# Storing the first output tile in four pieces as they are computed, in a SiLU-gate kernel

## The chip, the cores and the metric

The kernel runs on one core of a Trainium2 chip. The metric is the device time of one execution in microseconds (us), as the median of several executions. The span that a profile shows is about 1.8 us shorter than that time.

## The reference

```python
def setup_inputs():
    return {'x': np.random.randn(32, 512, 2048).astype(np.float32)}

def reference(x):
    half_dim = x.shape[-1] // 2
    x1, x2 = x[..., :half_dim].copy(), x[..., half_dim:].copy()
    silu_x1 = x1 * (1 / (1 + np.exp(-x1)))
    return (silu_x1 * x2).astype(np.float32)
```

There are 16384 rows of 8 KB that come in and 16384 rows of 4 KB that go out: 134.2 MB read and 67.1 MB written, with one SiLU and one multiply per output element.

## The kernel before

The rows are cut into 16 tiles. A tile gives each of the 128 partitions K = 8 neighbouring rows, so one partition's share of a load is one contiguous run of 64 KB in memory, and its share of a whole store is one run of 32 KB. There are two input buffers (`xt`) and two output buffers (`ot`). ScalarE (ACT) computes the SiLU, VectorE (DVE) the multiply, both in chunks of KC = 2 rows. ACT's queue issues the loads, SyncE's (SP) the stores. The last tile alone is stored chunk by chunk, in runs of 8 KB.

```python
    K = 8
    KC = 2
    ...
    in_pool = ctx.enter_context(tc.tile_pool(name="in_pool", bufs=2))
    out_pool = ctx.enter_context(tc.tile_pool(name="out_pool", bufs=2))
    ...
    def load(i):
        xt = in_pool.tile([P, K, in_cols], dt, name="xt")
        nc.scalar.dma_start(out=xt[:, :plan[i][1], :], in_=view(x_flat, i))
        loaded[i] = xt

    load(0)
    load(1)
    for i in range(n_tiles):
        k = plan[i][1]
        xt = loaded.pop(i)
        last = i == n_tiles - 1
        ov = view(out_flat, i)
        ot = out_pool.tile([P, K, half], dt, name="ot")
        for c in range(0, k, KC):
            ce = min(c + KC, k)
            nc.scalar.activation(out=ot[:, c:ce, :], in_=xt[:, c:ce, :half],
                                 func=mybir.ActivationFunctionType.Silu)
            nc.vector.tensor_mul(out=ot[:, c:ce, :], in0=ot[:, c:ce, :],
                                 in1=xt[:, c:ce, half:])
            if last:
                nc.sync.dma_start(out=ov[:, c:ce, :], in_=ot[:, c:ce, :])
        if not last:
            nc.sync.dma_start(out=ov, in_=ot[:, :k, :])
        if i + 2 < n_tiles:
            load(i + 2)
```

Load i+2 overwrites the input buffer of tile i, so it is issued when tile i has been computed. Tile i+2 writes the output buffer of tile i, so its first SiLU waits until store i has landed, all of it.

## Time and profile before

| | before |
|---|---|
| median time | 470.84 us (470.56 to 471.13, three runs) |
| span of the profiled execution | 468.9 us |
| one 64 KB load packet on one engine | 2.42 us |
| one 32 KB store packet | 1.21 us |
| one 8 KB store packet | 0.31 us |
| packets of one engine, added up at these durations | about 465 us |
| first tile's store: issued, landed | 32.7 us, 66.2 us |

Lines of the profile page of the kernel before. The DMA row gives the mean busy share of the 16 DMA engines in 40 slices of the span, in tenths; the line with percentages is the chain of waits by line; in the last three lines the numbers are the count, the size of each and the median time from issue to landing.

```profile
span 468.9 us, 269 instructions
...
DVE 142.3 (30%) x64; ACT 118.2 (25%) x65; POOL 0.2 (0%) x4
...
DMA  9899999999999998999999999999999989999998
...
DMA packets 5042, 201.35 MB, mean 429 GB/s; under 512 B 560, under 2 KB 560, under 8 KB 560
...
DMA xt<-in_x_dram 80%; DVE ot L92 15%; ACT ot L87 3%; DVEq L128 0%
...
out_dram<-ot SPq DMA_DIRECT2D x15, 4096.0 KB, 39.8
out_dram<-ot SPq DMA_DIRECT2D x4, 1024.0 KB, 5.7
xt<-in_x_dram ACTq DMA_DIRECT2D x16, 47.1
```

The engines that compute are idle for over two thirds of the span, and the DMA row has no hole. The kernel is bound by data movement. Reading the DMA row more finely: the trace has a record of each packet (start, duration, size, queue). The records do not name the engine, but each packet begins within some 4 ns of the end of another, so one engine's sequence can be followed from end to start. One DMA engine's packets, in order of time, look like this in the kernel before (L is the load queue, S the store queue, the number after it is the size in KB, the bracket is the duration in us):

```
38.88 S32(1.21)  40.09 L64(2.42)  42.50 S32(1.21)  43.72 S32(1.21)  44.93 L64(2.42)
47.34 S32(1.21)  48.55 L64(2.42)  50.96 S32(1.21)  52.17 L64(2.42)  54.59 S32(1.21)
```

Each packet starts when the one before it ends, and the two queues take turns, one packet each. (Where the store queue goes twice, at 42.50 and 43.72 us, a load had just ended: its 4-byte completion packet took the load queue's turn.)

Two more views of the kernel before: the waits (who waited for what; total us, times, longest us), and the timeline of tiles 0 to 2 (start, duration, instruction, count, and in brackets the idle time before it with what ended it; a line with x3 or x4 stands for several instructions, from the first one's start to the last one's end).

```profile
ACT ot L87 <- DMA xt<-in_x_dram: 338.8, 16, 22.1
DVE ot L92 <- ACT ot L87: 319.5, 16, 23.8
```

```profile
23.82 8.90 DVE L92 TENSOR_TENSOR ot<-ot,xt 128x2048 f32<-128x2048 f32 x4 [23.82 <-ACT ot L87]
32.74 51.99 SPq L100 DMA_DIRECT2D out_dram<-ot  x3
32.75 0.35 ACTq L74 DMA_DIRECT2D xt<-in_x_dram  x1
44.54 7.31 ACT L87 ACTIVATE ot<-xt 128x2048 f32<-128x2048 f32 x4 [15.36 <-DMA xt<-in_x_dram]
...
73.53 7.31 ACT L87 ACTIVATE ot<-xt 128x2048 f32<-128x2048 f32 x4 [21.68 <-DMA xt<-in_x_dram]
75.47 8.90 DVE L92 TENSOR_TENSOR ot<-ot,xt 128x2048 f32<-128x2048 f32 x4 [20.09 <-ACT ot L87]
84.40 0.37 ACTq L74 DMA_DIRECT2D xt<-in_x_dram  x1
```

ACT waits for loads alone, in all 16 tiles. Tile 2 starts at 73.53 us when its load lands; its output buffer has been free since 66.2 us.

### The profile page before, as it was taken

Reading aid. Unit: us, or ns where it says so; the run is one execution under the profiler, and the core shown is the slowest. Engines: PE = TensorE matmul, PEld = TensorE weight load, DVE = VectorE, ACT = ScalarE, POOL = GpSimd, SP = SyncE. Lnnn points to the kernel's source line nnn. Section 1 sums busy time; section 2 is a strip of 40 time slices with the busy share of each in tenths; the row PEclk is TensorE's granted clock in tenths of the full one; section 3 lists DMA queues with packets and bytes.
Section 4 is the critical chain, followed back from the end, with each engine's and each line's share of the span. In section 5 each row is a group of like instructions: output and inputs, shape, how many; then the busy total and the mean of one; then the engine's idle time right before and its main releaser. Section 6 shows DMA issues by size and latency. Waiting matters only on the chain.

```text
span 468.9 us, 269 instructions
## 1 busy us (share of the span) xinstructions
DVE 142.3 (30%) x64; ACT 118.2 (25%) x65; POOL 0.2 (0%) x4
## 2 busy tenths in 40 slices
DVE  0070705106061160601507025070250702407034
ACT  1142406023060330603206032060420604106051
POOL 0000000000000000000000000000000000000000
DMA  9899999999999998999999999999999989999998
GB/s 431 375 447 403 447 447 447 403 419 431 447 447 403 447 492 363 442 492 391 458 403 439 456 447 403 409 442 447 447 403 444 467 386 447 442 419 481 400 409 354
DMA packets 5042, 201.35 MB, mean 429 GB/s; under 512 B 560, under 2 KB 560, under 8 KB 560
## 3 DMA queue, kind: packets, MB, share of 16 engines
q10 hardware_dynamic: 2304, 134.22, 66.4%
q1 hardware_dynamic: 2736, 67.11, 33.2%
q14 instruction: 2, 0.02, 0.0%
HBM read 134.22 MB, written 67.11 MB: 429 GB/s over the span
## 4 chain that ended last, share of the span: by engine, by line
DMA 80%; DVE 15%; ACT 3%; DVEq 0%; issue 0%
DMA xt<-in_x_dram 80%; DVE ot L92 15%; ACT ot L87 3%; DVEq L128 0%
## 5 line engine op out<-in xcount | busy, mean ns | idle before, releaser
L92 DVE TENSOR_TENSOR ot<-ot,xt 128x2048 f32<-128x2048 f32 x64 | 142.3, 2286 | 319.5 <-ACT ot L87 319.5
L87 ACT ACTIVATE ot<-xt 128x2048 f32<-128x2048 f32 x64 | 116.9, 1897 | 338.8 <-DMA xt<-in_x_dram 338.8
L87 ACT ACT_TABLE_LOAD x1 | 1.3, 1283 | 1.3 <-PEq L117 1.3
L117 POOL MEMSET const-uint8-127<- 128x1 uint8 x1 | 0.1, 102 | 0.0
L117 POOL MEMSET const-bfloat16-1.0<- 128x1 bf16 x1 | 0.1, 101 | 0.0
L117 POOL MEMSET const-float32-0.0<- 128x1 f32 x1 | 0.1, 98 | 0.2 <-issue 0.2
L117 POOL MEMSET const-float32-1.0<- 128x1 f32 x1 | 0.1, 98 | 0.0
## 6 DMA issues: line engine op xcount, KB each, us to landing
out_dram<-ot SPq DMA_DIRECT2D x15, 4096.0 KB, 39.8
out_dram<-ot SPq DMA_DIRECT2D x4, 1024.0 KB, 5.7
xt<-in_x_dram ACTq DMA_DIRECT2D x16, 47.1
```

The source lines that it names most:

```text
L87: nc.scalar.activation(out=ot[:, c:ce, :], in_=xt[:, c:ce, :half], func=mybir.ActivationFunctionType.Silu,)
L92: nc.vector.tensor_mul(out=ot[:, c:ce, :], in0=ot[:, c:ce, :], in1=xt[:, c:ce, half:],)
L117: nc = _bacc.Bacc("TRN2", target_bir_lowering=False, num_devices=1)
```

## The change

The last tile's way of storing is used for the first tile too, so that the first store can begin at about 26 us, when two rows per partition are ready, and not at 32.7 us.

```diff
-        last = i == n_tiles - 1
+        in_pieces = i in (0, n_tiles - 1)
 [...]
-            if last:
+            if in_pieces:
                 nc.sync.dma_start(out=ov[:, c:ce, :], in_=ot[:, c:ce, :])
-        if not last:
+        if not in_pieces:
             nc.sync.dma_start(out=ov, in_=ot[:, :k, :])
```

## The prediction

> **What bounds the kernel now.** Data movement. The profile page's DMA row stands at 9 in nearly every slice, at a mean of 429 GB/s; DVE is busy 30%, ACT 25%; the chain of waits is 80% DMA of xt. The trace's DMA packet records say it more finely: a load moves 64 KB per packet (2.42 us on an engine), a tile store 32 KB (1.21 us), a last-tile piece 8 KB (0.31 us). Per engine that is 128, 120 and 32 packets: 309.5 + 145.6 + 9.9 = 465 us of a 468.9 us span. At most 4 us could be won, so a gain over 2% is out of reach.
>
> In steady state the two queues take strict turns, one load packet and one store packet, 3.63 us together: 2:1, just the ratio in which the kernel needs bytes. Both queues are always filled (a tile takes 29 us; a load lands after 47 us, a store after 40). The Trainium skill ("DMA: Bandwidth & Descriptors", section Queues, rings and completion order) says the engines go round robin between queues by packets of typically 9 to 17 descriptors. The trace agrees with the turns, but a turn here is one 64 KB or 32 KB run.
>
> **What the change does.** Bytes, compute (1.89 us per SiLU, 2.28 us per multiply) and instruction order on ACT and DVE stay. SP issues three more stores (0.33 us each, off the path). The first store can start at 26 us rather than 32.7. But the engines are full of loads then, so an early store only displaces a load.
>
> The harm: the pieces have 8 KB runs, so store 0 is 32 packets per engine instead of 8. If each turn is one packet, it gets 8 KB for every 64 KB of load. From about 31.5 us (3 packets left of load 1, 8 each of loads 2 and 3) there are 19 turns of 2.73 us, to about 84 us, with only 19 of 32 store packets out. The other 13 follow at 0.31 us. Store 0 lands at 88 to 91 us instead of 66.2.
>
> Tile 2 writes into tile 0's output buffer; the built program makes its first SiLU wait for all four pieces. Its input lands near 64 us, so ACT waits about 25 us, and load 4 cannot be issued. The load queue runs dry. Most of the stall is free: the loads ran ahead, and store 1 (8 x 1.21 = 9.7 us) then has the engines alone. After store 0 lands, tile 2 takes 10.9 us, and load 4 starts 1 to 2 us after issue. DMA idle: landing 0.5 to 2 + 10.9 + 1 to 2 - 9.7, so 2.7 to 5.2 us. Nothing later wins it back.
>
> **Predicted time: 474.3 us**, 80% range 470.4 to 477.2. Chances: faster by over 2% 0.01, within 2% 0.96, slower by over 2% 0.03.
>
> **What would show it right.** In the waits, one ACT wait of some 25 us for DMA out_dram at tile 2; store 0's last piece landing near 89 us; load 2 landing near 64 us rather than 73.5; one gap of 3 to 5 us without DMA packets near 98 to 103 us; the tail (last load's landing to the end, 17.9 us) about the same.
>
> **What would make it wrong.** If an engine sends several 8 KB packets in a turn, store 0 lands before load 3 ends, the load queue never dries up and the time stays at 470 to 471: about one chance in five. If restarting the queues costs more, it is above 477. If the stall brought a second one (tile 3 waiting for store 1), the gap would repeat; I count store 1 as landing just before it is needed.

## The result, and the profile after

The changed kernel takes 474.91 us (474.82 to 475.25, four runs) against 470.96 us (four runs) for the kernel before beside it. The ratio is 1.0086, with a 95% interval of 1.0069 to 1.0104: slower by 0.9%, within the 2% band, and clear of noise. Ratios here and below are the mean time of one kernel's fast runs over that of the other's in the same rounds, so not quite the ratio of the medians quoted.

Page lines of the kernel after, to be held against those of before:

```profile
span 473.5 us, 276 instructions
...
DVE 142.3 (30%) x64; ACT 118.2 (25%) x65; POOL 0.2 (0%) x4
...
DMA  9999998979999999999999999999999999999988
...
DMA packets 5474, 201.35 MB, mean 425 GB/s; under 512 B 608, under 2 KB 608, under 8 KB 608
...
DMA xt<-in_x_dram 69%; DVE ot L92 16%; ACT ot L87 4%; DVEq L128 0%; ACTq L74 0%; ACTq L87 0%
...
out_dram<-ot SPq DMA_DIRECT2D x14, 4096.0 KB, 46.9
out_dram<-ot SPq DMA_DIRECT2D x8, 1024.0 KB, 16.8
```

Compute and bytes are the same; there are 432 packets more; the DMA row has a 7 in its ninth slice, near 100 us. Its waits and its timeline at the same places:

```profile
ACT ot L87 <- DMA xt<-in_x_dram: 297.1, 14, 24.3
ACT ot L87 <- DMA out_dram<-ot: 40.0, 1, 40.0
ACT ot L87 <- DVE ot L92: 4.0, 1, 4.0
```

```profile
26.26 6.94 SPq L98 DMA_DIRECT2D out_dram<-ot  x4
32.87 0.37 ACTq L74 DMA_DIRECT2D xt<-in_x_dram  x1
43.44 7.31 ACT L87 ACTIVATE ot<-xt 128x2048 f32<-128x2048 f32 x4 [14.13 <-DMA xt<-in_x_dram]
...
54.31 0.37 ACTq L74 DMA_DIRECT2D xt<-in_x_dram  x1
90.76 7.31 ACT L87 ACTIVATE ot<-xt 128x2048 f32<-128x2048 f32 x4 [40.01 <-DMA out_dram<-ot]
92.70 8.90 DVE L92 TENSOR_TENSOR ot<-ot,xt 128x2048 f32<-128x2048 f32 x4 [38.42 <-ACT ot L87]
101.62 0.37 ACTq L74 DMA_DIRECT2D xt<-in_x_dram  x1
```

The first store is issued at 26.26 us, as intended. Its first packet starts only at 30.82 us, 4.6 us later (in the kernel before, issued at 32.74 us, it starts at 38.88): on full engines an earlier issue does not mean a packet at once. It lands far later than before: its four pieces land at 51.5, 73.4, 88.2 and 90.65 us. A new wait has appeared, ACT for the DMA of out_dram. The 40.0 us are ACT's whole idle time since tile 1; the load of tile 2 landed at 65.3 us, so the store alone is to blame for 25.4 us of them. Load 4 is issued at 101.62 us and not at 84.40.

The packet records of one engine show why the store is so late, and what the engine does about 100 us (same notation as above):

```
53.00 S8(0.31)  53.30 L64(2.42)  55.72 S8(0.31)  56.02 L64(2.42)  58.44 S8(0.31)  58.74 L64(2.42)
...
83.01 S8(0.31)  83.32 L64(2.57)  85.89 S8(0.31)  86.20 S8(0.31)  86.50 S8(0.31)  86.81 S8(0.31)
...
95.62 S32(1.21) 96.83 S32(1.21)  98.04 S32(1.21) 102.57 S32(1.93) 104.50 L64(3.27)
```

The turns are still one packet each, but a store packet now has 8 KB against 64 KB of a load. When load 3 has ended, at about 86 us, no load is left to send. The rest of store 0, then all of store 1, go out alone. From 99.97 to 102.45 us no engine has a packet: a gap of 2.48 us. The windows view shows that stretch (bounds and length, busy time of DVE, ACT and POOL with counts, clock, then DMA share and GB/s of the packets that start in the window):

```profile
97.50:100.00 2.50, 2.50 (x2) 0.56 (x1) 0.00 (x0) 1.00 0.52 223
100.00:102.40 2.40, 1.59 (x1) 0.31 (x1) 0.00 (x0) 1.00 0.00 0
102.40:105.00 2.60, 0.97 (x1) 2.60 (x2) 0.00 (x0) 1.00 1.97 605
```

Packets count where they start, so a window's share can be over 1; the 0 in the middle is the gap.

The sum closes. The last packet ends at 472.19 us against 467.62, 4.57 us later. Of this 2.48 us are the gap. The packets' durations, added and divided by 16 engines, grew by 1.63 us (466.57 to 468.20), and 1.48 us of that is in the first packets after the gap, which are long: 1.93 and 3.27 us above, where 1.21 and 2.42 us are usual. (Long 64 KB packets are not peculiar to a gap: the kernel before has 0.63 us of such excess per engine in its first 5 us, and 0.87 us at 35 to 40 us, just before its first store's packets begin.) The remaining 0.46 us fits the fact that the 2.48 us are only the time in which all 16 engines stand still together: taken one by one, the engines stop between 99.23 and 99.97 us and start again near 102.5 us, a pause of 3.0 us in the mean.

### The profile page after: what moved, and what is told of

Its sections match the earlier page's. It is cut to its first block, busy times and chain, and to the rows that moved or that the text cites. A ratio compares the mean times of both kernels' runs of the same rounds, so it can differ in the third digit from the quotient of the medians.

```text
span 473.5 us, 276 instructions
## 1 busy us (share of the span) xinstructions
DVE 142.3 (30%) x64; ACT 118.2 (25%) x65; POOL 0.2 (0%) x4
## 4 chain that ended last, share of the span: by engine, by line
DMA 69%; DVE 16%; another core or an unknown queue 8%; ACT 4%; DVEq 0%; issue 0%; ACTq 0%
DMA xt<-in_x_dram 69%; DVE ot L92 16%; ACT ot L87 4%; DVEq L128 0%; ACTq L74 0%; ACTq L87 0%
```

## The experiments

The theory: **small packets in a one-for-one turn make store 0 late; tile 2 must wait for its buffer; the load queue runs dry; the engines have a gap.** Rival 1: the early start itself harms, as an early store displaces loads. Rival 2: more DMAs or small packets cost engine time as such. All kernels below gave correct results. "Gap" is a stretch in which none of the 16 engines has a packet in progress, from the packet records of the profiled execution. Four chips were used, one each for late8k to eight4k, for tile8 to fine, for fine_whole to fine_two16k, and for fine_silu; each had the kernel before beside it, so the ratios can be held against each other, the medians less so. The diffs of late8k to eight4k are against the kernel before, the others against the change.

| label | tile 0 stored as | median us | before us | ratio (95% interval) | gap us | store 0 landed |
|---|---|---|---|---|---|---|
| (the change) | 4 early, 8 KB runs | 474.91 | 470.96 | 1.0086 (1.0069, 1.0104) | 2.48 | 90.7 |
| late8k | 4, 8 KB, written after the loop | 475.05 | 470.95 | 1.0093 (1.0079, 1.0107) | 2.48 | 92.7 |
| late32k | 4 late, 32 KB | 471.87 | 470.95 | 1.0038 (1.0007, 1.0068) | none | 72.5 |
| two16k | 2 early, 16 KB | 470.95 | 470.95 | 1.0000 (0.9988, 1.0012) | none | 81.1 |
| eight4k | 8 early, 4 KB | 475.75 | 470.95 | 1.0100 (1.0087, 1.0113) | 2.53 | 91.5 |
| tile8 | whole; tile 8 in 4 | 475.40 | 470.76 | 1.0095 (1.0081, 1.0109) | 2.48 | 66.8 |
| tile13 | whole; tile 13 in 4 | 471.13 | 470.76 | 1.0004 (0.9991, 1.0016) | none | 67.4 |
| all8k | every tile in 4 | 477.21 | 470.76 | 1.0131 (1.0114, 1.0149) | none | 90.2 |
| fine | as the change, waits by region | 479.26 | 470.76 | 1.0177 (1.0163, 1.0191) | none | 90.4 |
| fine_whole | whole, waits by region | 470.88 | 471.19 | 0.9995 (0.9983, 1.0008) | none | 66.5 |
| silu_early | as the change | 472.91 | 471.19 | 1.0037 (1.0025, 1.0049) | 0.56 | 90.3 |
| fine_two16k | as two16k, waits by region | 470.97 | 471.19 | 1.0001 (0.9987, 1.0016) | none | 80.8 |
| fine_silu | as fine | 471.52 | 470.93 | 1.0010 (0.9997, 1.0023) | none | 91.4 |

### Small pieces, meant to start late: late8k

```diff
             if last:
                 nc.sync.dma_start(out=ov[:, c:ce, :], in_=ot[:, c:ce, :])
-        if not last:
+        if i == 0:
+            for c in range(0, k, KC):
+                nc.sync.dma_start(out=ov[:, c:c + KC, :], in_=ot[:, c:c + KC, :])
+        elif not last:
```

> The four 8 KB-run pieces of tile 0 are all issued after tile 0 is computed, so nothing starts early. Theory (small packets in a one-for-one turn, so store 0 is late, tile 2 waits for its buffer, the load queue runs dry): still slow, 474 to 476 us, store 0 landing at 88 to 92 us and one DMA gap of 2.5 to 4 us near 100 us. Rival 1 (an early store displaces loads): 470.5 to 471.5 us, like the kernel before.

This run did not do what its label says: the pieces are written after the loop, but the built program issued them at 26.6, 28.8, 31.0 and 33.2 us, as early as in the change, since SyncE waits for nothing but the multiply that each piece needs. So it is a repetition of the change under another spelling (475.05 us, gap 2.48 us), and it says nothing about rival 1. A run with 8 KB pieces that do start late was not made. (The gap, 2.48 us, and the landing of store 0, 92.7 us, lie just outside the ranges expected.) The profiled execution, at 477.2 us, was 2 us above the other five.

### More DMAs without small packets: late32k

```diff
-        if not last:
+        if i == 0:
+            for p in range(0, P, 32):
+                nc.sync.dma_start(out=ov[p:p + 32], in_=ot[p:p + 32, :k, :])
+        elif not last:
```

> Tile 0 is stored in four DMAs, after it is computed, but cut by partitions (32 each), so that a run stays 32 KB. Theory: as the kernel before, 470.3 to 471.5 us, store 0 landed by 67 us, no gap. Rival 2 (four DMAs instead of one cost their fixed time or their semaphores): 472 to 476 us.

It came out at 471.87 us, 0.9 us above the kernel before, with no gap; one of its six runs was at 476.6 us and widens the interval. The expectation missed by 0.4 us, so that the time lies between the two ranges, a little below that of rival 2; and store 0 landed at 72.5 us, not by 67. The records show two things: each of the four DMAs ends with a completion packet that takes a store turn, so three load packets more (3 x 2.42 = 7.3 us) go ahead of store 0, and 0.9 us of lengthened 32 KB packets lie at 65 to 70 us. Four DMAs instead of one are thus not quite free here: by the medians about a quarter of the change's 3.95 us. The interval, which the run at 476.6 us widens, reaches 0.68%, so this run alone does not rule rival 2 out; tile13 below, with four DMAs of small packets and no loss, does.

### Early, with half the packets: two16k

```diff
+            elif i == 0 and ce % 4 == 0:
+                nc.sync.dma_start(out=ov[:, ce - 4:ce, :], in_=ot[:, ce - 4:ce, :])
-        if not last:
+        if i > 0 and not last:
```

> Tile 0 is stored early, in two pieces of 4 rows (16 KB runs, 16 packets per engine). Theory: 16 turns of 2.42 + 0.61 us from about 34 us, store 0 lands near 80 to 82 us, ACT waits some 12 us for it, but the load queue is refilled just as store 1 ends: gap under 1 us, 470.0 to 471.6 us. Rival 1 (early start): 473 us or more, as the early start is kept. Rival 2 (a cost for each piece): about a third of the loss, 472.3.

The time is that of the kernel before, to 0.01 us. The store starts early here (28.45 us, not 32.7), without a loss, so an early start alone does no harm: rival 1 is out. It still lands late, at 81.1 us, and tile 2 still waits for it:

```profile
81.17 7.31 ACT L87 ACTIVATE ot<-xt 128x2048 f32<-128x2048 f32 x4 [29.05 <-DMA out_dram<-ot]
83.11 8.90 DVE L92 TENSOR_TENSOR ot<-ot,xt 128x2048 f32<-128x2048 f32 x4 [27.46 <-ACT ot L87]
92.04 29.26 SPq L102 DMA_DIRECT2D out_dram<-ot  x2
92.04 0.37 ACTq L74 DMA_DIRECT2D xt<-in_x_dram  x1
```

Tile 2's load had landed at 69.0 us, so ACT waited 12 us for the store, as expected. This wait costs nothing, and neither do those that follow: the twelve tiles after it each wait 13 to 14 us for a store beyond the landing of their load. Load 4 is issued at 92.04 us, 9.6 us earlier than in the change, and the engines had packets without a break. (The expectation had load 4 come just as store 1 ends. It came sooner, before load 3 had landed at 95.7 us, so the load queue did not run dry.) In these runs a late store cost time when it came late enough to empty both queues.

### Twice the small packets: eight4k

```diff
+            elif i == 0:
+                for r in range(c, ce):
+                    nc.sync.dma_start(out=ov[:, r:r + 1, :], in_=ot[:, r:r + 1, :])
-        if not last:
+        if i > 0 and not last:
```

> Tile 0 is stored early in eight pieces of 1 row (4 KB runs, 64 packets per engine): twice the small packets of the change. Theory: once the load queue has run dry the rest of store 0 goes at full rate, so the gap does not grow: 474 to 476.5 us, store 0 landing at 89 to 92 us, gap 2.5 to 4 us. Rival 2 (a cost for each small packet or DMA): twice the loss or more, 478.5 us or above.

475.75 us, as the theory expected: 64 packets per engine for store 0 instead of 32 leave the gap at 2.53 us. A cost for each packet would have doubled the loss; it is 4.8 us instead of 3.95.

The run is not a clean doubling, though. The built program held back some of the DMAs until earlier ones had landed, as the waits of SP's queue show for the seventh and the eighth piece:

```profile
SPq L101 <- DMA xt<-in_x_dram: 10.7, 1, 10.7
SPq L101 <- DMA out_dram<-ot: 7.3, 1, 7.3
```

Load 3 too was issued only at 64.73 us (54.31 in the change), after the second piece had landed at 64.65 us. The load queue was empty for 4.8 us there, and about half of the 64 small packets went out in that time, not in turns with loads. So store 0 landed at 91.5 us, inside the range expected, but not in the way expected. By the theory the gap needs only that store 0 lands when load 3 has ended (it landed at 89.8 us) and that load 4 waits for it, and this was so here too. Against a cost for each packet the run counts in full: store 0 had twice the packets.

### Another tile: tile8 and tile13

```diff
-        in_pieces = i in (0, n_tiles - 1)
+        in_pieces = i in (8, n_tiles - 1)       # tile13: i in (13, n_tiles - 1)
```

> Tile 8 is stored in four 8 KB-run pieces instead of tile 0. Theory: nothing is special about the first tile; store 8 is late, tile 10 waits for its buffer, one gap of 2.5 to 4 us near 330 us, 474 to 476 us. Rival (a matter of the ramp-up, where loads run ahead of stores): 470.5 to 471.5.

> Tile 13 is stored in four 8 KB-run pieces instead of tile 0. Its late store holds up tile 15 only, and after load 15 there is no load to come that the wait could delay. Theory: the load queue has nothing to lose, so no gap above 1 us before the last store: 470 to 472 us. A rival that charges small packets as such expects 474 to 475, as for tile 0.

Tile 8 costs what tile 0 costs (475.40 us); the gap has moved with it. Windows of tile8:

```profile
330.50:333.00 2.50, 2.50 (x2) 0.55 (x1) 0.00 (x0) 1.00 0.34 144
333.00:335.40 2.40, 1.58 (x1) 0.32 (x1) 0.00 (x0) 1.00 0.00 0
335.40:338.00 2.60, 0.98 (x1) 2.60 (x2) 0.00 (x0) 1.00 1.97 605
```

So the start of the program has no part in it. With tile 13 the same pieces, started as early, cost nothing (471.13 us):

```profile
449.44 7.31 ACT L87 ACTIVATE ot<-xt 128x2048 f32<-128x2048 f32 x4 [21.21 <-DMA out_dram<-ot]
```

ACT waits for the store here too, 6.7 us beyond the landing of its load at 442.7 us (the 21.21 us are again its whole idle time). That is less than the change's 25.4 us, as one load fewer takes turns with the store; and no load is left that the wait could delay.

### Every tile in pieces: all8k

```diff
-        in_pieces = i in (0, n_tiles - 1)
+        in_pieces = True
```

> All 16 tiles are stored in four 8 KB-run pieces. A simple rival, a loss for each tile stored so, gives 15 times 4 us, about 530 us. Theory: while one late store drains, the next one is just as full of small packets, so the engines have store work while tile i+2 is computed (9.9 us against about 13) and a gap comes at most once in a while; by counting turns I expect 472 to 478 us, with ACT waiting over 10 us for stores at about every second tile, yet few gaps.

477.21 us, in the range; fifteen times the change's loss is nowhere near. ACT waits for stores 11 times (297.7 us of idle time in total; nine times over 10 us beyond the landing of the load, near the every second tile expected), and no gap is left: the load queue is empty for up to 19.1 us at a time, but small store packets are then still there to send. (SP held stores back as well, 13 times, until earlier ones had landed.) The profiled execution has 6.0 us more of packet durations per engine: 2.8 us because four 8 KB packets (4 x 0.309 us) take a little longer than one of 32 KB (1.213 us), which makes a difference of 0.023 us in 15 tiles with 8 such fours each, and the rest in packets that took longer than usual, most of them 64 KB ones.

### The wait cut by region: fine and fine_whole

Both output buffers become halves of one allocation. The built program then makes each SiLU of tile 2 wait only for the piece whose rows it overwrites. The DMAs are the same.

```diff
-    out_pool = ctx.enter_context(tc.tile_pool(name="out_pool", bufs=2))
+    out_pool = ctx.enter_context(tc.tile_pool(name="out_pool", bufs=1))
+    ot_both = out_pool.tile([P, 2 * K, half], dt, name="ot")
 [...]
-        ot = out_pool.tile([P, K, half], dt, name="ot")
+        ot = ot_both[:, (i % 2) * K:(i % 2) * K + K, :]
```

> The same early 8 KB pieces as the change, but both output buffers are halves of one allocation, so that the built program makes each SiLU of tile 2 wait only for the piece whose rows it overwrites. The DMA traffic is the same. Theory: tile 2 is computed row pair by row pair while store 0 goes out, load 4 is issued at 94 to 97 us instead of 101.6, before store 1 ends: the gap shrinks to under 1 us, 470.0 to 471.7 us, although store 0 still lands near 90 us. If the small packets themselves cost the time (in turns or on the engines), it stays at 474 to 475.

The wait did what was expected: tile 2 was computed piece by piece, load 4 was issued at 94.64 us, there is no gap. The time did not: 479.26 us, worse than the change. The packet records show a cost that had not been there: in every tile from 100 us on, a number of 64 KB packets take 2.5 to 3.3 us instead of 2.42, 6.1 us more per engine over the span than in the kernel before, and the engines drift out of step until the first and the last end the same DMA 4.9 us apart. In the kernel before they keep within 0.4 us up to 280 us and within 0.9 us to the end.

The control is the same allocation with tile 0 stored whole (the diff above, and `in_pieces = i == n_tiles - 1`).

> Control for the run fine, which came out slower (479.3 us) though its gap was gone: both output buffers are halves of one allocation as there, but tile 0 is stored whole as in the kernel before. If the allocation itself (its place, its semaphores) slowed the load packets of fine: 476 us or more. If it took the allocation together with the late store of small pieces: 470.3 to 471.6 us, like the kernel before.

470.88 us, so the allocation by itself is innocent. The expectation for fine failed, then, and the run alone neither confirms nor refutes the theory: it took the gap away and brought another cost. So the gap was narrowed by another way.

### The gap made narrower: silu_early

Tile 2 alone writes its SiLU into its own input buffer, so ACT needs no output buffer and only the multiplies wait.

```diff
         ot = out_pool.tile([P, K, half], dt, name="ot")
+        act = xt[:, :, :half] if i == 2 else ot
 [...]
-                out=ot[:, c:ce, :],
+                out=act[:, c:ce, :],
 [...]
-                in0=ot[:, c:ce, :],
+                in0=act[:, c:ce, :],
```

> The change, with the SiLU of tile 2 alone written in place into its input buffer, so that it runs while store 0 still drains; only its multiplies wait for the output buffer. The DMA traffic and the buffers are those of the change. Theory (the gap is the time from store 0's landing to load 4's first packet, less store 1's 9.7 us): load 4 is issued about 2 us earlier, near 99.6 instead of 101.6 us, the gap shrinks from 2.5 to 0.3 to 0.8 us, and the time falls to 472.5 to 473.5 us. A theory in which the small packets or the slow turns cost the time themselves: 474.5 to 475.5, unchanged.

Each number came out:

```profile
99.34 0.36 ACTq L74 DMA_DIRECT2D xt<-in_x_dram  x1
```

Load 4 is issued at 99.34 us instead of 101.62, the gap is 0.56 us instead of 2.48, and the time is 472.91 us, 1.7 us over the kernel before beside it, where the change was 3.95 us over. The store is as late as ever (90.3 us) and its packets are the same. Its windows, beside those of the change above:

```profile
97.50:100.00 2.50, 1.80 (x1) 0.02 (x1) 0.00 (x0) 1.00 0.49 210
100.00:102.40 2.40, 0.47 (x1) 2.40 (x2) 0.00 (x0) 1.00 2.10 655
102.40:105.00 2.60, 2.60 (x2) 2.60 (x2) 0.00 (x0) 1.00 0.00 0
```

(The last 0 is no gap: the long first load packets, 3.2 us, started in the window before and still run.) What is left, 1.7 us, is of the size of the rest of the gap (0.56 us) and the long first packets (1.41 us per engine), 2.0 us together.

### The side effect of fine: fine_two16k and fine_silu

fine_two16k is fine with the pieces of two16k. fine_silu is fine with the in-place SiLU of silu_early in tiles 2 and 3.

> The allocation of fine with tile 0 stored early in two 16 KB-run pieces. Without fine's side effect: 470.3 to 471.7 us, no gap, as two16k. If the region-by-region waits bring the slowed load packets of fine by themselves, whatever the piece size: 475 us or more, with 64 KB packets over 2.6 us in every tile.

> The run fine (early 8 KB pieces, waits by region) with the SiLU of tiles 2 and 3 also written in place into their input buffers, so that loads 4 and 5 can be issued some 2 us earlier than in fine. Theory of the change: no gap, so whatever is not the side effect of fine is 470.3 to 471.7 us. About that side effect: in fine every store ended 3.6 us after a load, one turn, and the load packets just after were slow; in all fast kernels it ended at another distance. If that distance matters, this run is at 470.3 to 471.7 us when the distance comes out as another one, and slow (over 475) when it stays 3.6 us. If early small pieces with waits by region are slow at any distance: over 475 us with another distance.

fine_two16k is at 470.97 us (one of six runs at 473.0), without the slow packets. fine_silu is at 471.52 us, the median of seven; one of them, at 478.6, counts as slow and is left out of the ratio, and the profiled one was at 473.7 us. There the stores ended 7 to 8 us after a load and not 3.6 us, and the lengthening of the 64 KB packets had shrunk from 6.1 to 1.0 us above before. In most of its runs, then, early small pieces came with next to no loss when the engines never ran out of packets (the load queue alone was empty for 10.8 us), which fits the theory from the other side; but the run at 478.6 us, with no profile, is as slow as fine and may have had its side effect. What makes the packets of fine slow stays open: its distance of 3.6 us between a load's end and a store's end is the only one of its kind among these runs, but one kernel at that distance does not show that it is the cause. The drift of the engines is not enough to explain it: in fine_silu they end the same DMA over 4 us apart as well.

## Why the prediction was right

- **Bound by data movement, so no gain over 2%.** Right: none of the thirteen other kernels was faster than the kernel before by more than the noise, and the DMA engines of the kernel before have no gap.
- **One packet per turn whatever its size.** Right, and it was the step that could have failed (the prediction gave it one chance in five). The records show 8 KB and 64 KB in alternation for as long as there are loads. two16k and eight4k show the same with 16 KB and 4 KB. Of the 32 packets of store 0 per engine, about 12 were left when the loads had ended; the prediction had 13.
- **Store 0 at 88 to 91 us, load 2 near 64 us.** Measured 90.65 and 65.3 us.
- **Tile 2 waits about 25 us for its output buffer.** 25.4 us beyond the load. The waits view says 40.0, since it counts from the end of tile 1; the prediction should have said which of the two it meant.
- **The gap of 2.7 to 5.2 us** (3 to 5 in the list of what to look for). Measured 2.48 us, slightly below both. The terms, for the engine that ended last: landing 0.36 us after its last packet of store 0 (90.65 against 90.29), 10.97 us from landing to the next issue, 0.83 us from issue to the first packet, less 9.68 us of store 1. The landing term (0.5 to 2 us) and the issue term (1 to 2 us) were both sized too large.
- **Restart.** The prediction put a costlier restart under what could go wrong. A cost was there that the sum did not have: the packets after the gap were 1.48 us longer in sum. The gap sized too large and the cost left out nearly cancelled in the total: +3.5 us predicted (474.3 against 470.84), +3.95 us measured. The mechanism was right; that the total came this close is luck.
- **The tail "about the same".** Wrong. The last load's landing to the end is 20.2 us, against 17.9 us: the last load came only 2.3 us later than before, and stores were further behind when it did. With full engines this only moves work between the two queues; two16k has a tail of 24.1 us and loses nothing.
- **No second stall.** Right: tile 3 waited 4.0 us for DVE, not for store 1, which had landed at 100.33 us.

Of the causes tried, the early start (two16k, tile13), the number of DMAs (tile13; late32k, all but about 0.9 us) and the number of small packets (tile13, eight4k) were refuted as the main one; the gap was moved (tile8), narrowed (silu_early) and removed (two16k, tile13, fine_silu), and the time followed in each of these. In fine and all8k the gap was gone too and the time rose, by packets that took longer: in fine for a reason that stays open.

## What to carry to other kernels

When two DMA queues are both full, ask how long one contiguous run of each is, and not only how many bytes each has: here the queues took turns by run, so cutting a store's runs to an eighth of the load's starved that store. In these runs a late store was free until its buffer held up a load long enough to empty both queues; cost such a store as the time in which neither queue has anything to send, not as the length of the wait that the profile shows. Where the DMA engines were busy for the whole span, starting a transfer earlier gained nothing (two16k).

## What the Trainium skill lacked or had wrong

- "DMA: Bandwidth & Descriptors", Queues, rings and completion order: the round robin by packets is as the page says, but its typical packet of 9 to 17 descriptors is not what a turn was here. A turn was one contiguous run, of 64, 32, 16, 8 or 4 KB (2.42, 1.21, 0.61, 0.31 and 0.16 us). That two queues therefore share the engines in the ratio of their run lengths is on no page.
- The same page, Rules for kernel authors, gives 128 partitions and at least 1 MiB per DMA for maximum bandwidth. The pieces of the change keep this rule (1 MiB each) and still cost 0.9%; the rule says nothing of a second queue with longer runs. The 8 KB runs were not slow in themselves: 4 x 0.309 us against 1.213 us for 32 KB.
- The same page, Why a DMA increments its semaphore by 16 and not by 1, tells that each engine's share of a DMA ends with a semaphore write; it does not say that this packet (4 bytes, 9 ns) uses up a turn. In late32k three more of them put some 7.3 us of loads ahead of the store (landed at 72.5 us instead of 66.2).
- The same page, Where 436 GB/s comes from, says that the HBM side (about 358 GB/s) binds transfers between HBM and SBUF, though it has a measured 425 GB/s on one core beside it. The sentence lacks the condition that the page gives under its measured table, that about 358 GB/s is what a core gets when both cores of a pair stream. This program, on one core, moved 429 GB/s over its whole span, and 64 KB in 2.418 us on 16 engines is 434 GB/s, near the page's fabric figure of 435.
- No page has the cost of a restart: after a gap of 2.48 us the first packets took up to 2.0 us (32 KB) and 3.4 us (64 KB), 1.48 us more than usual in the sum per engine; after one of 0.56 us it was nearly the same (1.41 us). That the pause causes this is not shown: late32k has 0.90 us of lengthened 32 KB packets at 65 to 71 us without any gap.
- No page explains the lengthened load packets of fine (6.1 us per engine, engines up to 4.9 us out of step), and these runs do not either.
